# A 31-tap depthwise convolution: five of eight channel tiles moved from VectorE, ScalarE and GpSimd to TensorE as two-phase Toeplitz products

## The chip, the cores and the metric

The kernel runs on one core of one Trainium2 chip. The metric is the device time of one execution of the whole program in microseconds (us). TensorE is PE (its weight loads are PEld), VectorE is DVE, ScalarE is ACT, GpSimd is POOL, and SyncE (SP) issues most of the transfers.

## What is computed

The program is a whole stack of layers on 512 tokens with a model width of 1024: one hybrid layer, then feed-forward layers and two other mixers. Only the hybrid layer is touched. Cut to what matters:

```python
def causal_depthwise_conv(u, w, b):                  # 31 taps, each channel for itself
    y = lax.conv_general_dilated(u, w[:, None, :], window_strides=(1,),
        padding=[(CONV_SIZE - 1, 0)], dimension_numbers=("NWC", "WIO", "NWC"), feature_group_count=c)
    return y + b

def hybrid_layer(x, ...):
    h = rms_norm(x, pre_g)
    proj = jnp.einsum("bld,de->ble", h, w_in)
    conv_in, z_c, u_s, z_s, g_c, g_s = jnp.split(proj, IN_OFFSETS, axis=-1)
    ca, cb = jnp.split(conv_in, 2, axis=-1)
    cu = causal_depthwise_conv(ca * jax.nn.sigmoid(cb), conv_w, conv_b)
    cu = jax.nn.silu(layer_norm(cu, conv_ln_g, conv_ln_b))
    conv_out = jnp.einsum("blc,cd->bld", cu * jax.nn.silu(z_c), w_conv_out)
    y = jax.nn.gelu(s5_mimo(u_s, ...))               # a state-space scan, 32 groups
    y = y * jax.nn.sigmoid(jnp.einsum("blc,ce->ble", y, w_glu) + b_glu)
    ssm_out = jnp.einsum("blc,cd->bld", y * jax.nn.silu(z_s), w_ssm_out)
    merged = jax.nn.sigmoid(g_c) * conv_out + jax.nn.sigmoid(g_s) * ssm_out
    return x + rms_norm(jnp.einsum("bld,de->ble", merged, w_out), post_g)
```

All of it is float32. A float32 product on PE is made as three products of rounded halves: high by high, low by high and high by low.

## The kernel before

Channels lie on the 128 partitions and the 512 tokens on the free axis, so the 1024 conv channels are eight tiles of 128x512. The hybrid layer is `block1` (L598).

**Projections.** `wload` (L211) brings weights in pieces of 128x1024: SP issues a transfer of 512 KB into `raw` (L219; two buffers), ACT rounds it into `wh` (L220), and DVE subtracts to get `wl` (L221), with two buffers each. `mm3` (L226) then issues eight times the three products L232, L233, L234 for a piece, each 128x512, so a piece is 24 products. `proj(i)` makes two output tiles from two pieces.

**The conv.** For a tile, `pair` (L666) projects both halves and writes the gated input `cu` with 30 zeros ahead of it. `conv` (L683) has two forms. Tiles 0, 3, 4 and 5 (`CONV_POOL`) go to ACT and POOL: for each of the 30 further taps ACT makes `cw` (the shifted input times one weight, L689; two buffers), and POOL adds it to the sum (L690). Tiles 1, 2, 6 and 7 go to DVE: one multiply (L692) and 30 multiply-adds (L695). POOL sums the finished tiles into `sacc` (L699, L701). The layer norm starts with a PE product of `sacc` (L765, `ln`).

**The state-space scan (S5).** Tables come first on DVE (L342, L453, L457), then for each of four quarters `s5_pre` (Q: powers by L506 to L511 on DVE, products of tables on POOL at L488 and L491, small fp32 products on PE) and `s5_main` (q: PE products L556, L560, L568, L578, L579, with the scan L562 to L574 on DVE between them).

**What sets the order.** `run` (L800) walks two strings, ORDER_A (L902) and ORDER_B. A letter is a step and a digit its number: p is `pair`, c is `conv`, u, s and z are other projections, Q and q the scan, y the GELU behind it, g the gates, G the GLU, L the layer norm, S and C the two output products. B1_PRIO gives the conv (class C) a priority number 20000 higher, that is, the scheduler treats it as a filler. A list scheduler then fixes one static order for every engine; every engine works its list strictly in that order.

```python
ORDER_A = "p0 p1 T z0 c1 u0 u1 s0 p2 Q0 Q1 q0 c2 c0 p3 c3 s1 Q2 q1 p4 z1 Q3 q2 p5 p7 z2 q3 c5 c7 c4 p6 c6 z3"
ORDER_B = "y0 g0 g1 g2 y1 y2 y3 g3 G L g4 g5 g6 S0 g7 S1 C0 C1 C2 C3 C4 C5 C6 C7"
```

Of the kernel before, what the change touches and what calls it, by code (L numbers as in the profile page):

```python
# [1921 lines left out]
```

## Time and profile before

| | |
|---|---|
| three runs | 2721.5, 2722.85, 2728.67 us (median 2722.85) |
| the profiled execution | span 2722.4 us; no time of its own is listed beside the span |
| PE busy | 2562.2 us (94%) |
| DVE busy | 1551.5 us (57%) |
| ACT busy | 937.7 us |
| POOL busy | 593.6 us |
| transfers | 241.33 MB, 89 GB/s |

The hybrid layer takes the first 640 us or so of the span. The profile is one execution as the hardware recorded it. Busy time of PE is modelled from pipelined instructions, so the distance between the starts of products tells more than their durations. "x120" is a count, the number behind it a mean in ns, and "idle ... <-" the time an engine stood still ahead of such instructions and who ended it.

### The profile page before, as it was taken

Reading aid. Unit: us, or ns where it says so; the run is one execution under the profiler, and the core shown is the slowest. Engines: PE = TensorE matmul, PEld = TensorE weight load, DVE = VectorE, ACT = ScalarE, POOL = GpSimd, SP = SyncE. Lnnn points to the kernel's source line nnn. Section 1 sums busy time; section 2 is a strip of 40 time slices with the busy share of each in tenths; the row PEclk is TensorE's granted clock in tenths of the full one; section 3 lists DMA queues with packets and bytes.
Section 4 is the critical chain, followed back from the end, with each engine's and each line's share of the span. In section 5 each row is a group of like instructions: output and inputs, shape, how many; then the busy total and the mean of one; then the engine's idle time right before and its main releaser. Section 6 shows DMA issues by size and latency. Waiting matters only on the chain.

```text
span 2722.4 us, 31415 instructions
## 1 busy us (share of the span) xinstructions
PE 2562.2 (94%) x12356; PEld 2034.6 (75%) x12356; DVE 1551.5 (57%) x2148; ACT 937.7 (34%) x1337; POOL 593.6 (22%) x407
## 2 busy tenths in 40 slices
PE   6676778998999999999999999999999999999999
PEld 4565656887888876787678888888888666788887
DVE  9999897646434458653564344443444755643442
ACT  5343445443222333222243233322223554422231
POOL 5787765013000044432010000100001321100000
PEclk8888878998999999899999999999999989999999
DMA  3222112332222242213122322322324312122323
GB/s 112 68 64 64 58 63 81 105 112 70 96 98 101 91 146 64 65 57 111 63 93 90 104 93 92 102 99 88 104 88 134 118 41 66 55 95 88 106 94 106
DMA packets 113189, 241.33 MB, mean 89 GB/s; under 512 B 43856, under 2 KB 52688, under 8 KB 113040
## 3 DMA queue, kind: packets, MB, share of 16 engines
q1 hardware_dynamic: 112784, 238.52, 26.9%
q8 instruction: 97, 1.59, 0.2%
q0 software_dynamic: 256, 0.80, 0.1%
q14 instruction: 52, 0.43, 0.1%
HBM read 224.72 MB, written 13.37 MB: 87 GB/s over the span
## 4 chain that ended last, share of the span: by engine, by line
PE 77%; DVE 17%; issue 2%; DMA 1%; ACT 1%; POOL 1%; SPq 0%; DVEq 0%; ACTq 0%; POOLq 0%
PE bank L232 22%; PE bank L234 22%; PE bank L233 22%; DVE xa L695 4%; PE bank L1797 2%; DVE wl L221 2%; DVE s5x L342 1%; DVE kt L530 1%; ACT wh L220 1%; POOL acc L249 1%; PE bank L1349 1%; PE bank L1153 0%; DMA raw<-in_ffn_dn_dram 0%; DVE ra L509 0%; DVE s5t L342 0%
## 5 line engine op out<-in xcount | busy, mean ns | idle before, releaser
L234 PE MATMUL bank<-xh,wl 128*128 128x512 f32 (+1 forms) x2144 | 855.2, 399 | 69.7 <-DVE wl L221 69.3
L232 PE MATMUL bank<-xh,wh 128*128 128x512 f32 (+1 forms) x2144 | 849.1, 397 | 25.2 <-ACT wh L220 14.8
L233 PE MATMUL bank<-xl,wh 128*128 128x512 f32 (+1 forms) x2144 | 850.8, 397 | 15.7 <-DVE xl L851 6.9
L220 ACT CAST wh<-raw 128x1024 fp32r<-128x1024 f32 (+1 forms) x432 | 416.0, 964 | 1174.4 <-PE bank L233 941.4
L221 DVE TENSOR_TENSOR wl<-raw,wh 128x1024 fp32r<-128x1024 f32 (+2 forms) x398 | 459.6, 1156 | 385.7 <-ACT wh L220 384.4
L234 PEld LDWEIGHTS bank<-xh,wl 128*128 128x128 f32 x2144 | 414.1, 193 | 172.7 <-DVE wl L221 78.1
L232 PEld LDWEIGHTS bank<-xh,wh 128*128 128x128 f32 x2144 | 413.7, 193 | 119.2 <-ACT wh L220 19.9
L233 PEld LDWEIGHTS bank<-xl,wh 128*128 128x128 f32 x2144 | 414.2, 193 | 109.7 <-DVE xl L851 7.8
L249 POOL TENSOR_TENSOR acc<-acc,sq 128x512 f32<-128x512 f32 x54 | 81.5, 1509 | 1263.9 <-ACT sq L248 1263.0
L234 PE MATMUL bank<-mh,wl 128*128 128x512 f32 x704 | 274.4, 390 | 0.6 <-DVE wl L221 0.6
L233 PE MATMUL bank<-ml,wh 128*128 128x512 f32 x704 | 274.3, 390 | 0.0
L232 PE MATMUL bank<-mh,wh 128*128 128x512 f32 x704 | 274.1, 389 | 0.0
L308 DVE TENSOR_TENSOR up<-bank,rs 128x512 f32<-128x512 f32 x88 | 60.8, 691 | 267.2 <-PE bank L234 267.2
L690 POOL TENSOR_TENSOR xa<-xa,cw 128x512 f32<-128x512 f32 x120 | 191.3, 1595 | 56.4 <-ACT cw L689 51.7
L304 DVE TENSOR_TENSOR gp<-bank,rs 128x512 f32<-128x512 f32 x88 | 60.7, 690 | 180.1 <-PE bank L234 180.0
L234 PEld LDWEIGHTS bank<-mh,wl 128*128 128x128 f32 x704 | 132.1, 188 | 33.7 <-DVE wl L221 2.0
L233 PEld LDWEIGHTS bank<-ml,wh 128*128 128x128 f32 x704 | 132.2, 188 | 27.8
L232 PEld LDWEIGHTS bank<-mh,wh 128*128 128x128 f32 x704 | 132.2, 188 | 25.6
L695 DVE SCALAR_TENSOR_TENSOR xa<-cu,hcw,xa 128x512 f32<-128x512 f32 x120 | 141.8, 1181 | 1.6
L689 ACT ACTIVATE cw<-cu,hcw 128x512 f32<-128x512 f32 x120 | 85.3, 720 | 90.1 <-POOL xa L690 89.9
L221 POOL TENSOR_TENSOR wl<-raw,wh 128x1024 fp32r<-128x1024 f32 x34 | 82.7, 2434 | 145.9 <-ACT wh L220 145.4
L238 ACT CAST mh<-m 128x512 fp32r<-128x512 f32 x88 | 54.9, 624 | 60.8 <-DVE m L310 60.8
(636 smaller groups left out, 2836.7 us busy)
## 6 DMA issues: line engine op xcount, KB each, us to landing
raw<-in_ffn_gu_dram SPq DMA_DIRECT2D x176, 512.0 KB, 3.6
raw<-in_ffn_dn_dram SPq DMA_DIRECT2D x64, 512.0 KB, 3.5
raw<-in_w_in_dram SPq DMA_DIRECT2D x46, 512.0 KB, 3.6
raw<-in_even_in_dram SPq DMA_DIRECT2D x26, 512.0 KB, 3.6
raw<-in_ffn_dn_dram SPq DMA_DIRECT2D x64, 192.0 KB, 3.2
xa<-in_xT_dram SPq DMA_DIRECT2D x16, 256.0 KB, 4.4
raw<-in_w_co_dram SPq DMA_DIRECT2D x8, 512.0 KB, 3.3
raw<-in_w_out_dram SPq DMA_DIRECT2D x8, 512.0 KB, 3.5
```

The lines of the kernel that those rows point to most:

```text
L220: nc.scalar.copy(h[:, :m], raw[:, :m])
L221: self.wlo.tensor_tensor(out=l[:, :m], in0=raw[:, :m], in1=h[:, :m].bitcast(F32), op=ALU.subtract)
L232: self.nc.tensor.matmul(ps, h[i][:, s], xh[k], start=a, stop=False)
L233: self.nc.tensor.matmul(ps, h[i][:, s], xl[k], start=False, stop=False)
L234: last = self.nc.tensor.matmul(ps, l[i][:, s], xh[k], start=False, stop=b)
L238: self.nc.scalar.copy(hi, src)
L249: nc.gpsimd.tensor_tensor(out=acc, in0=acc, in1=sq, op=ALU.add)
L304: nc.vector.tensor_tensor(out=gp, in0=pg, in1=rs, op=ALU.mult)
L308: nc.vector.tensor_tensor(out=up, in0=pu, in1=rs, op=ALU.mult)
L689: A.activation(w, cu[:, j:j + T], AF.Copy, scale=hcw[:, 31 * k + j:31 * k + j + 1])
L690: GP.tensor_tensor(out=y, in0=y, in1=w, op=ALU.add)
L695: STT(out=y, in0=cu[:, j:j + T], scalar=hcw[:, 31 * k + j:31 * k + j + 1], in1=y, op0=ALU.mult, op1=ALU.add)
```

## The change

Tiles 1, 2, 4, 6 and 7 (`CONV_PE`) get their convolution from PE; tiles 0, 3 and 5 stay on ACT and POOL; DVE convolves nothing. For a tile on PE the tokens are split into even and odd ones (two phases), and 64 channels by two phases fill the 128 partitions. A tap pair is then a 128x128 matrix whose four blocks are diagonal: 16 such matrices for each group of 64 channels, 32 for a tile. The host lays them out as a new input `conv2` of 5x128x4096 floats (10.5 MB more to load).

- `phases(k)` (step P) does what `pair` did, with four 64x256 multiply-adds on DVE that write the two-phase layout `cp`, then a rounding on ACT (`cph`), a subtraction on DVE (`cpl`) and two small clears on POOL.
- `toeplitz(k)` (step t, class V, priority 0) loads four pieces of 128x1024 of `conv2` through the same `wload`, issues 96 products of 128x256 into a PSUM bank of its own (`cv`), and ACT writes the result back to token order in four 64x256 pieces.
- z2 and z3 move from ORDER_A to the front of ORDER_B; the side banks go from four to three; buffers of `zp` go from 12 to 8 with four in a new pool, and `CU_BUFS` from 3 to 2.

```diff
+CONV_PE = (1, 2, 4, 6, 7)
+        P.use_banks(mm=4, sd=3, cv=1)
+        def phases(k):
+            ...
+            cp = m_("cp")
+            va, cc = (x.rearrange("p (k o) -> p o k", o=2) for x in (vb, ca))
+            for g in range(2):
+                for o in range(2):
+                    gs = slice(64 * g, 64 * g + 64)
+                    STT(out=cp[64 * o:64 * o + 64, 256 * g:256 * g + 256], in0=va[gs, o], scalar=1.0, in1=cc[gs, o],
+                        op0=ALU.add, op1=ALU.mult)
+            hi, lo = (cup.tile([128, 2, 272], R, name=n, tag="cph", bufs=4) for n in ("cph", "cpl"))
+            for t in (hi, lo):
+                GP.memset(t[:, :, 0:16].bitcast(F32), 0.0)
+            c3 = cp.rearrange("p (g k) -> p g k", g=2)
+            A.copy(hi[:, :, 16:], c3)
+            TT(out=lo[:, :, 16:], in0=c3, in1=hi[:, :, 16:].bitcast(F32), op=ALU.subtract)
+            cus[k] = hi, lo
+        def toeplitz(k):
+            (hi, lo), y = cus[k], yc[k]
+            ps = P.bank("cv")
+            src = ap["conv2"][CONV_PE.index(k)]
+            for c in range(4):
+                (h,), (l,) = P.wload(src[:, 1024 * c:1024 * c + 1024], 1024)
+                g, s0 = c // 2, 8 * (c % 2)
+                for i in range(8):
+                    s = 16 - s0 - i
+                    o = slice(128 * i, 128 * i + 128)
+                    ...
+                    xh, xl = hi[:, g, s:s + 256], lo[:, g, s:s + 256]
+                    nc.tensor.matmul(d, h[:, o], xh, start=a, stop=False)
+                    nc.tensor.matmul(d, h[:, o], xl, start=False, stop=False)
+                    nc.tensor.matmul(d, l[:, o], xh, start=False, stop=b)
+            y3 = y.rearrange("p (k o) -> p o k", o=2)
+            for g in range(2):
+                for o in range(2):
+                    ps_ = slice(64 * o, 64 * o + 64)
+                    A.activation(y3[64 * g:64 * g + 64, o], ps[ps_, 256 * g:256 * g + 256], AF.Identity, scale=0.5, ...)
+            summed(k)
-ORDER_A = "p0 p1 T z0 c1 u0 u1 s0 p2 Q0 Q1 q0 c2 c0 p3 c3 s1 Q2 q1 p4 z1 Q3 q2 p5 p7 z2 q3 c5 c7 c4 p6 c6 z3"
-ORDER_B = "y0 g0 g1 g2 y1 y2 y3 g3 G L g4 g5 g6 S0 g7 S1 C0 C1 C2 C3 C4 C5 C6 C7"
-CU_BUFS = 3
-CONV_POOL = (0, 3, 4, 5)
+ORDER_A = "p0 P1 T z0 c0 u0 u1 s0 p3 t1 Q0 Q1 q0 c3 P2 t2 s1 Q2 q1 p5 z1 c5 P4 t4 Q3 q2 P6 t6 q3 P7 t7"
+ORDER_B = "z2 z3 y0 g0 g1 g2 y1 y2 y3 g3 G L g4 g5 g6 S0 g7 S1 C0 C1 C2 C3 C4 C5 C6 C7"
+CU_BUFS = 2
+CONV_POOL = (0, 3, 5)
```

The lines of the scan functions stand 15 lower in the new file (L221 is L236, L690 is L759). Up to the layer norm the PE list has 36 pieces of projections and GLU from u0 on in both kernels, and the new one has 20 pieces of `conv2` besides.

**TensorE, the seam between the projection of tile 7 and its convolution (step P7 to t7), in the new list.** `xh` and `xl` are the rounded halves of the layer's input, bank_80 is `cv`:

```order
L249 MATMUL bank_76<-xh_98,wl 128x512
L247 MATMUL bank_76<-xh_99,wh 128x512
L248 MATMUL bank_76<-xl_107,wh 128x512
L249 MATMUL bank_76<-xh_99,wl 128x512
L741 MATMUL bank_80<-cph,wh 128x256
L742 MATMUL bank_80<-cpl,wh 128x256
L743 MATMUL bank_80<-cph,wl 128x256
```

The first Toeplitz product stands directly behind the last projection product that its own input is made from; the 96 of tile 7 are followed by z2.

**VectorE, the scan of the first quarter (q0), before.** The scan is `vr`, `vs`, `st` (later `sh`); `xa` is the conv's output:

```order
L562 TENSOR_TENSOR vr<-bank_79,rsn 128x512
L563 TENSOR_TENSOR vs<-vs,rc 128x512
L695 SCALAR_TENSOR_TENSOR xa<-cu,hcw,xa 128x512
L221 TENSOR_TENSOR wl<-raw,wh 128x1024
L564 TENSOR_TENSOR vs<-vs,vr 128x512
L695 SCALAR_TENSOR_TENSOR xa<-cu,hcw,xa 128x512
L530 SCALAR_TENSOR_TENSOR kt<-ident,s5d,kt 16x16 x4
L566 SCALAR_TENSOR_TENSOR st_1229<-d_1202,vs 128x512
L695 SCALAR_TENSOR_TENSOR xa<-cu,hcw,xa 128x512 x2
L221 TENSOR_TENSOR wl<-raw,wh 128x1024
L695 SCALAR_TENSOR_TENSOR xa<-cu,hcw,xa 128x512
L678 SCALAR_TENSOR_TENSOR cu<-vb,bank_75 128x512
```

**The same place in the new list:**

```order
L545 SCALAR_TENSOR_TENSOR kt<-ident,s5d,kt 16x16 x4
L236 TENSOR_TENSOR wl<-raw,wh 128x1024 x2
L577 TENSOR_TENSOR vr<-bank_79,rsn 128x512
L578 TENSOR_TENSOR vs<-vs,rc 128x512
L579 TENSOR_TENSOR vs<-vs,vr 128x512
L581 SCALAR_TENSOR_TENSOR st_1945<-d_1918,vs 128x512
L236 TENSOR_TENSOR wl<-raw,wh 128x1024
L697 SCALAR_TENSOR_TENSOR cu<-vb,bank_75 128x512
L587 TENSOR_TENSOR vr<-bank_77,rsn 128x8x63
L588 TENSOR_TENSOR st_1945<-st_1945,rc 128x8x63
L515 MEMSET rsn 128x8
L589 TENSOR_TENSOR sh<-st_1945,vr 128x8x63
```

The conv's multiply-adds are gone from between the scan's steps. Splits of weights (L236) stand there, and the scan runs to its end (`sh`, which PE waits for) within these rows.

**ScalarE, the middle of the scan of the first quarter, before:**

```order
L689 ACTIVATE cw<-cu,hcw 128x512 x3
L220 CAST wh<-raw 128x1024
L689 ACTIVATE cw<-cu,hcw 128x512
L527 COPY kt<-bank_77 16x512
L689 ACTIVATE cw<-cu,hcw 128x512
L220 CAST wh<-raw 128x1024
L689 ACTIVATE cw<-cu,hcw 128x512
L675 ACTIVATE vb<-bank_76 128x512
L517 COPY m_1667<-bank_78 128x512
L689 ACTIVATE cw<-cu,hcw 128x512
L686 ACTIVATE xa<-cu,vec,hcw 128x512
L689 ACTIVATE cw<-cu,hcw 128x512 x2
```

**In the new list, from the load of the projection for P2:**

```order
L235 CAST wh<-raw 128x1024
L758 ACTIVATE cw<-cu,hcw 128x512 x4
L235 CAST wh<-raw 128x1024
L712 ACTIVATE vb<-bank_76 128x512
L532 COPY m_1869<-bank_77 128x512
L758 ACTIVATE cw<-cu,hcw 128x512 x2
L532 COPY m_1869<-bank_78 128x512
L724 CAST cph<-cp 128x2x256
L758 ACTIVATE cw<-cu,hcw 128x512 x5
L596 COPY yq<-bank_79 128x512
L758 ACTIVATE cw<-cu,hcw 128x512
L235 CAST wh<-raw 128x1024
```

In both lists roundings of weights (`wh`) stand behind runs of one to five `cw`; in the new one the tanh (L712) and rounding (L724) of `phases` stand among them too.

## Rows read from the trace of the kernel before

**Rows 1.** The page, parts 1 and 2: busy time of the engines; VectorE in 40 slices.

```profile
PE 2562.2 (94%) x12356; PEld 2034.6 (75%) x12356; DVE 1551.5 (57%) x2148; ACT 937.7 (34%) x1337; POOL 593.6 (22%) x407
...
DVE  9999897646434458653564344443444755643442
```

**Rows 2.** Windows: us, PE, PEld, DVE, ACT, POOL busy, clock, DMA share, GB/s.

```profile
59.40:140.30 80.90, 56.10 (x217) 43.12 (x217) 80.90 (x148) 28.44 (x38) 58.94 (x40) 0.82 0.22 71
...
237.00:290.30 53.30, 38.47 (x177) 30.98 (x176) 49.20 (x66) 23.21 (x36) 41.58 (x33) 0.81 0.21 60
...
374.20:444.00 69.80, 55.31 (x222) 44.66 (x222) 62.16 (x56) 36.68 (x57) 42.78 (x27) 0.83 0.24 80
...
59.40:444.00 384.60, 286.38 (x1192) 223.66 (x1192) 364.38 (x484) 160.02 (x229) 285.18 (x188) 0.84 0.21 65
444.00:608.00 164.00, 160.63 (x731) 131.73 (x729) 86.20 (x104) 70.54 (x98) 22.55 (x14) 0.98 0.30 103
```

**Rows 3.** Timeline of PE around 444: start, us, instruction.

```profile
443.98 1.02 PE L765 MATMUL bank<-sacc,ones 128*128 128x512 f32 x2
```

**Rows 4.** Groups of instructions, 59.4 to 444 us: busy, mean ns, idle before.

```profile
L690 POOL TENSOR_TENSOR xa<-xa,cw 128x512 f32<-128x512 f32 x120 | 191.3, 1595 | 56.4 <-ACT cw L689 51.7
L695 DVE SCALAR_TENSOR_TENSOR xa<-cu,hcw,xa 128x512 f32<-128x512 f32 x120 | 141.8, 1181 | 1.6
L234 PE MATMUL bank<-xh,wl 128*128 128x512 f32 x281 | 125.4, 447 | 64.6 <-DVE wl L221 64.6
...
L221 DVE TENSOR_TENSOR wl<-raw,wh 128x1024 fp32r<-128x1024 f32 x38 | 58.8, 1548 | 10.5 <-ACT wh L220 10.5
L220 ACT CAST wh<-raw 128x1024 fp32r<-128x1024 f32 x37 | 38.5, 1040 | 48.1 <-PE bank L233 33.3 <-DVE xa L695 7.2 <-DMA raw<-in_w_in_dram 4.9
L488 POOL TENSOR_TENSOR t<-s5bb,s5t 128x512 f32<-128x512 f32 x8 | 23.0, 2891 | 2.1 <-PE bank L516 2.1
...
L578 PE MATMUL bank<-us,tz 128*128 128x64 f32 x64 | 14.6, 316 | 2.6 <-ACT kt L527 2.6
...
L508 DVE TENSOR_TENSOR rc<-ra 128x8 f32<-128x8 f32 (+5 forms) x24 | 14.1, 594 | 0.3
...
L488 POOL TENSOR_TENSOR w<-s5c,s5t 128x576 f32<-128x576 f32 x6 | 8.5, 1436 | 0.0
L507 DVE TENSOR_TENSOR ra<-rsn,s5t 128x8 f32<-128x8 f32 (+5 forms) x24 | 7.7, 323 | 0.0
```

**Rows 5.** The conv's output tiles, 59 to 444 us: duration ns min/median/max.

```profile
L690 POOL TENSOR_TENSOR xa<-xa,cw x120: 1260/1597/4583, 64.0 to 436.8; 128x512 f32<-128x512 f32 x120
L695 DVE SCALAR_TENSOR_TENSOR xa<-cu,hcw,xa x120: 712/752/1897, 73.0 to 429.9; 128x512 f32<-128x512 f32 x120
```

**Rows 6.** The split weights, same stretch: duration ns min/median/max.

```profile
L221 DVE TENSOR_TENSOR wl<-raw,wh x38: 1205/1215/2305, 60.9 to 442.5; 128x1024 fp32r<-128x1024 f32 x38
```

**Rows 7.** Window of the conv's VectorE line L695 alone: us, DVE busy.

```profile
59.40:140.30 80.90, 30.33 (x30) 0.82 0.22 71
```

**Rows 8.** Timeline of PE: 512- and 256-column products.

```profile
594.91 0.39 PE L234 MATMUL bank<-xh,wl 128*128 128x512 f32 x1
595.14 0.28 PE L232 MATMUL bank<-xh,wh 128*128 128x256 f32 x1
595.25 0.28 PE L233 MATMUL bank<-xl,wh 128*128 128x256 f32 x1
```

**Rows 9.** Groups by form, 600 to 640 us: half-size tiles on ACT and DVE.

```profile
L851 DVE SCALAR_TENSOR_TENSOR xl<-xa,vec,xh 128x256 fp32r<-128x256 f32 x16 | 9.3, 605 | 2.5 <-ACT xh L850 2.5
...
L850 ACT ACTIVATE xh<-xa,vec 128x256 fp32r<-128x256 f32 x16 | 8.1, 505 | 11.5 <-POOL xa L848 11.5
```

**Rows 10.** Waits, 59.4 to 444 us: total, times, longest.

```profile
ACT cw L689 <- POOL xa L690: 89.9, 58, 8.8
...
POOL xa L690 <- ACT cw L689: 51.7, 18, 10.0
```

**Rows 11.** The page, part 6: transfers of weights; KB each, us to landing.

```profile
raw<-in_w_in_dram SPq DMA_DIRECT2D x46, 512.0 KB, 3.6
```

More of the change, by code (lines that the diff above doesn't have):

```diff
@@ L92, in pack @@
     put("invf", np.tile(invf, 4)[:, None])
+    cw = a["conv_w"][0].reshape(31, 8, 2, 64)
+    two = np.zeros((8, 2, 64, 2, 16, 2, 64), np.float32)
+    ch = np.arange(64)
+    for pi in range(2):
+        for po in range(2):
+            for s in range(16):
+                lag = 2 * s + po - pi
+                if 0 <= lag <= 30:
+                    two[:, pi, ch, :, s, po, ch] = cw[30 - lag].transpose(2, 0, 1)
+    f["conv2"] = two.reshape(8, 128, 4096)[list(CONV_PE)]
+    for k in range(8):
+        for g in range(2):
+            cb = a["conv_b"][0][128 * k + 64 * g:128 * k + 64 * g + 64]
+            vec[:, VEC["cb2"][0] + 2 * k + g] = np.concatenate([cb, cb])
     f["vec"] = vec
@@ L627, in z_, with y_ @@
             return zp.tile([128, T], dt, name=name, tag="z")
+        def y_(name, dt=F32):
+            return pools["z"].tile([128, T], dt, name=name, tag="z")
         def m_(name):
@@ L681, in block1 @@
         ndone = []
+        def phases(k):
+            if k < RAW:
+                (pa, pb), ca = pre[k], m_("ca")
+                vb = m_("vb")
+                TT(out=vb, in0=pb, in1=rs, op=ALU.mult)
+                A.activation(vb, vb, AF.Tanh, scale=0.5)
+                TT(out=ca, in0=pa, in1=rs, op=ALU.mult)
+            else:
+                ca, pb = proj(k)
+                vb = m_("vb")
+                A.activation(vb, pb, AF.Tanh, scale=0.5)
+            cp = m_("cp")
[12 more added lines that the diff above has]
+            cus[k] = hi, lo
@@ L717, in zc_ @@
             for a, ps in enumerate(proj(12 + i)):
-                z = z_("zc")
+                z = (z_ if i < 2 else y_)("zc")
                 A.activation(z, ps, AF.Silu)
@@ L776, in ln @@
                 TT(out=yc[k], in0=yc[k], in1=zc[k], op=ALU.mult)
-                f = z_ if k < 6 else c
+                f = z_ if k < 4 else y_ if k < 6 else c
                 a, b = f(f"cah{k}", R), f(f"cal{k}", R)
@@ L792, in block1 @@
         tb = {}
-        step = {"p": pair, "c": conv, "u": u_, "s": zs_, "z": zc_, "g": gate, "y": gelu,
+        step = {"p": pair, "c": conv, "P": phases, "t": toeplitz, "u": u_, "s": zs_, "z": zc_, "g": gate, "y": gelu,
                 "Q": lambda q: s5_pre(P, tb, q), "q": lambda q: s5_main(P, tb, q, u_dram, y_dram),
@@ L1883, in odd @@
         P.use_banks(mm=4, sd=4)
-_ORDER = ["xT", "vec", "w_in", "w_co", "w_so", "w_glu", "w_out", "s5p", "s5bc", "s5d", "ffn_gu", "ffn_dn",
+_ORDER = ["xT", "vec", "conv2", "w_in", "w_co", "w_so", "w_glu", "w_out", "s5p", "s5bc", "s5d", "ffn_gu", "ffn_dn",
           *EVEN_IN, *ODD_IN]
```

17 lines of the change are left out of this document (13 added, 4 removed).

## The prediction, made before the changed kernel was run

> **What bounds the kernel now.** I read the page first: PE is busy 94% of the span, but VectorE stands at nine tenths or more in the first slices and at half of that later [rows 1]. So the hybrid layer has a limit of its own, and PE's 94% is an average over others. Then the table of windows: from 59.4 us (the first piece of u0) to 444 us DVE is busy 364.4 of 384.6 us, while PE has gaps and a granted clock of 0.84; from 444 to 608 us PE is busy 160.6 of 164 us at 0.98 [rows 2]. The border is the layer norm's PE product [rows 3]: in front of it DVE sets the pace, behind it PE. In the groups the conv is DVE's largest line, 141.8 us, and PE stood idle 64.6 us ahead of L234 for DVE's split `wl` [rows 4]. So a conv multiply-add that leaves DVE lets the splits come earlier, and PE's time up to 444 us is what the change can move. What stands behind the norm is the same work in both kernels, limited by PE already, and keeps its length.
>
> The sum therefore asks one thing: when is the norm's product reached? It is made against the profiled execution, span 2722.4 us; the page gives no other time of it, and the median of the runs is 0.45 us higher. A measurement of this kernel tells about 0.3%, 8 us, from no change.
>
> **DVE and POOL part by part.** DVE loses 120 multiply-adds, 141.8 us, and 4 starts. It gains 20 splits, between 1.2 us (the fastest [rows 6]) and 1.55 us (the mean [rows 4]), so 24 to 31 us; 20 multiply-adds of 64x256, for which no row exists: the half tile of 128x256 took 0.605 us [rows 9], half that would be a floor, I take 0.5 us, 10 us in all (less five `cu` that fall away); and five subtractions, 3 us. Net it loses about 105 us. POOL loses 30 adds, ACT 30 `cw`. ACT gains 20 roundings of 1.04 us [rows 4], 20 evictions and 5 roundings at 0.5 us [rows 9]; at 160 of 384.6 us busy [rows 2] it is not the limit by its sum.
>
> An add on POOL takes 1.595 us in the mean, 1.26 at best; the multiply-add on DVE 1.181 in the mean, 0.712 at best [rows 4, 5]. Both are long while the other runs. With DVE's conv gone I take the middle for the add, 1.43 us, and keep 1.26 and 1.595 as ends.
>
> **PE.** Products of 512 columns start 0.227 us apart at full clock; two 256-column products, each with another weight, 0.11 us apart (0.12 over a longer stretch) [rows 8]. I take 0.12 us. Five tiles of 96 make 480 products, 58 us. The 36 other pieces up to the norm are 864 products, 196 us, in both kernels. The scan's small products I put at 60 us in both: some 260 records at the 0.23 us of L578 [rows 4]. So PE's work up to the norm rises from 256 to 314 us at full clock, with 384.6 us in which to do it before. That alone does not forbid a gain, but leaves at most 70 us of it.
>
> **The sum by stretches of the new order.** In each I price every engine and take the busiest; durations as above, the scan's POOL operations (46 in six lines, means from 1.44 to 2.89 us [rows 4]) at 1.8 us, the powers on DVE (six lines of 24, means 0.32 to 0.59 us [rows 4]) at 0.46 us.
> - u0 u1 s0 p3 (8 pieces): DVE was busy all 80.9 us of this stretch, 30.3 of them the conv [rows 2, 7]. Without these 50; but 72 powers stand here instead of 31: 41 x 0.46 = 19. DVE 69, POOL 17 x 1.43 + 16 x 1.8 = 53, PE 192 x 0.227 + 1.5 = 45. **69.**
> - t1 P2 t2 (10 pieces): POOL 28 x 1.43 + 16 x 1.8 + 3 = 72; PE 48 x 0.227 + 192 x 0.12 + 21 of scan = 55; DVE some 55. **72.**
> - s1 p5 z1 P4 (8): PE 43.6 + 17 = 61; POOL 51; DVE 40. **61.**
> - t4 P6 (6): PE 10.9 + 11.5 + 14 = 36; POOL 30. **36.**
> - t6 P7 t7 (10): PE 10.9 + 23 + 7 = 41, and two places where the first Toeplitz product waits for its own input: tanh, four multiply-adds, rounding, subtraction, 0.6 + 2 + 0.5 + 0.6 us and the hand-overs, 4.5 us each. **50.**
> - z2 z3 g0 to g3, GLU (14): 336 x 0.227 = 76, at PE's share behind the norm (160.6 of 164 [rows 2]) **78.**
>
> The first four are 238 us. Two corrections have opposite signs. Engines wait for each other: stretches in which DVE was not quite full took 53.3 us for 49.2 of its work and 69.8 for 62.2 [rows 2], 8 and 12% more. But the lists run over the borders, and over the four stretches no engine has more than 200 us (PE 197). I take neither. The norm is then reached at 59.4 + 238 + 50 + 78 = 425 us in place of 444, 19 us earlier: 2722.4 - 19 = **2704 us** (about 0.7% faster).
>
> The 10.5 MB of `conv2` cost nothing by bandwidth: transfers take 0.21 of the DMA engines there [rows 2]. By latency they have no slack: 3.6 us to land [rows 11], 1.04 to round, 1.2 to 1.55 to split, over two buffers, is about 3.0 us per piece, and PE eats a Toeplitz piece in 24 x 0.12 = 2.9 us. z2 and z3 cost nothing by moving: PE has them behind t7 with nothing else to wait for. The two small clears of `phases` on POOL and the third side bank I also put at nothing; POOL's slack in the last two stretches covers the clears.
>
> **The rivals.**
>
> 1. *It gains more, 2682 us.* If the lists overlap well, the four stretches take half-way between the largest sum of one engine (197) and 238, 218 us; the norm comes 39 us earlier with 50 and 78 as above, and 40 if the two waits shrink a little. For it: DVE no longer fills any stretch but the first. Against: PE's 314 us of work would have to fit into 345 (0.91), where before 256 took 384.6 (0.67) and my own sum has 366 (0.86).
>
> 2. *POOL and DVE take turns, 2740 us, slower.* The distance between best and mean on both engines [rows 5] can be read so that one of the two stands whenever the other reads two tiles. Then their times add: 88 adds at 1.26 (111), 46 scan operations at 1.44 (66), 32 splits at 1.2 (39), 148 powers at 0.32 (48) and some 10 us of the scan make 274 us for the four stretches in place of 238, and the norm comes at 461, 17 us late. It decides from a sum above 257, where the norm is where it was. Against it: the same sum before is 120 x (1.26 + 0.712) + 66 + 38 x 1.2 + 46 + 10 = 404 us, which did not fit into the 384.6 us that it took, so at least 20 us did overlap; and the median multiply-add took 0.752 us [rows 5], hardly more than the fastest.
> The Trainium skill, page "SBUF — State Buffer", section "Who interferes with whom", states this rule: a VectorE instruction with two SBUF inputs contends with a GpSimd instruction that reads SBUF, and who comes second is blocked for the whole instruction. The long instructions here agree with it, the 404 us do not agree with its strict form. By the rule the time would be rival 2's, and three conv tiles that stay on POOL would keep the new splits waiting.
>
> 3. *ACT's list starves PE, 2753 us, slower.* ACT's `cw` already waits 89.9 us for POOL [rows 10], and in the new list weight roundings stand behind up to five `cw`. Five adds on POOL are 8 us, a Toeplitz piece only 2.9, and there are two buffers. If waiting costs the worst ratio above in all four stretches (12%, 29 us) and every one of the 20 Toeplitz pieces comes 1 us late, that is 49 us against my sum, 30 us slower than before. Against it: POOL has fewer adds, and ACT has slack.
>
> 4. *Gain and loss cancel, about 2723 us.* Waiting at 8% in the four stretches takes back 19 us exactly. That the change would not do what it says I count here: the new lists show no conv instruction on DVE and all 480 Toeplitz products, so hardly 1 in 100.
>
> **How the numbers follow.** My forecast has a chance of 0.42, rival 1 0.08, rival 4 0.20, rival 2 0.17, rival 3 0.13. So faster 0.50, same 0.20, slower 0.30. Cases of both signs hold the chance; the forecast's own range is 2694 to 2714: adds at 1.26 us in the second stretch (5 us less) and splits at 1.2 us in the first and third (5 less) below, waits of 4% in the four stretches (10 us) above. The range for 8 in 10 reaches from 5 us under rival 1 (those adds again), 2677, to just above rival 3, 2757.
>
> **What would show it.** Right: DVE no longer near full between 59 and 425 us; L759 (the adds) nearer to 1.4 than 1.6 us; Toeplitz products 0.12 us apart at full clock within a piece; the norm's product, now L838, near 425 us; the 164 us behind it unchanged. The sum by stretches is wrong if z2 is reached much later than 347 us (59.4 + 238 + 50), and the place where PE stands then names the rival: for `wl` behind long splits, rival 2; for `wh` behind `cw`, rival 3. Wrong altogether would be a stretch behind the norm that changed its length.

## The result and the profile after

The changed kernel takes 2733.48 us (median of 6 runs) against 2721.78 us of before (6 runs): slower by some 12 us. The recorded ratio is 1.0052 with the interval 1.0033 to 1.007 (the medians alone give 1.0043). The forecast was 2704 us, faster; the wide range held the time, the sign was wrong. The profiled execution is the slowest of the six runs (2744.4 us, span 2742.7), 11 us above their median, while the profiled execution of before lies 1 us above its own; so the two profiles differ by 20 us where the medians differ by 12. Where I compare traces I look at single stretches and waits.

The page: busy time, then VectorE in 40 slices.

```profile
span 2742.7 us, 32329 instructions
...
PE 2610.5 (95%) x12836; PEld 2092.4 (76%) x12836; DVE 1447.9 (53%) x2064; ACT 950.4 (35%) x1351; POOL 511.4 (19%) x382
...
DVE  9967643636434448743464344443444755643443
```

Against [rows 1] PE has 48 us more, DVE 104 us and POOL 82 us less. The first slices of DVE are still at nine tenths. The timeline of PE shows the norm's product:

```profile
461.77 1.02 PE L838 MATMUL bank<-sacc,ones 128*128 128x512 f32 x2
```

It starts 17.8 us later than in [rows 3]; behind it the span has 2280.9 us left, before 2278.4. So the loss stands where the prediction put the gain, ahead of the norm. The windows of the six stretches (each runs from the rounding of its first piece to that of the next stretch's), then the whole up to the norm and a window of 164 us behind it; columns as in [rows 2]:

```profile
59.40:137.50 78.10, 52.90 (x207) 41.14 (x207) 77.17 (x171) 29.16 (x38) 54.57 (x42) 0.80 0.23 72
137.50:217.60 80.10, 60.63 (x343) 51.68 (x341) 57.66 (x83) 38.55 (x57) 62.81 (x51) 0.79 0.27 80
217.60:269.70 52.10, 52.10 (x266) 42.83 (x265) 33.35 (x40) 31.02 (x44) 43.79 (x34) 1.00 0.32 96
269.70:317.80 48.10, 35.62 (x212) 30.40 (x211) 38.10 (x49) 25.57 (x40) 34.14 (x28) 0.82 0.27 77
317.80:382.30 64.50, 51.63 (x292) 45.92 (x291) 31.67 (x43) 22.36 (x33) 6.73 (x6) 0.81 0.36 107
382.30:461.80 79.50, 79.50 (x364) 66.29 (x364) 23.26 (x23) 27.21 (x37) 1.29 (x1) 1.00 0.31 106
59.40:461.80 402.40, 332.38 (x1674) 278.26 (x1674) 261.22 (x405) 173.87 (x245) 203.33 (x160) 0.87 0.29 90
461.80:625.80 164.00, 157.46 (x733) 130.35 (x731) 89.58 (x108) 74.34 (x106) 28.14 (x21) 0.99 0.31 103
```

By these the stretches took 78, 80, 52, 48, 65 and 80 us, where the sum had 69, 72, 61, 36, 50 and 78; the third, 9 us shorter, hid a part of what the others lost. z2 is reached at 382 us in place of 347. DVE is full in the first stretch only. In the second no engine is above 63 of 80 us. The clock is granted fully (2.4 GHz) in the third and the last and is at 0.79 to 0.82 in the other four; if only 2.4 and 1.2 GHz occur, that is some 40% of them at 1.2 GHz. The groups, 59.4 to 461.8 us (busy, mean ns, idle before):

```profile
L759 POOL TENSOR_TENSOR xa<-xa,cw 128x512 f32<-128x512 f32 x90 | 129.1, 1435 | 55.1 <-ACT cw L758 52.5
L249 PE MATMUL bank<-xh,wl 128*128 128x512 f32 x281 | 113.9, 405 | 25.2 <-DVE wl L236 25.2
...
L236 DVE TENSOR_TENSOR wl<-raw,wh 128x1024 fp32r<-128x1024 f32 x58 | 81.0, 1397 | 107.3 <-ACT wh L235 107.3
...
L741 PE MATMUL bank<-cph,wh 128*128 128x256 f32 x160 | 51.0, 319 | 14.8 <-ACT cph L724 14.8
...
L521 DVE TENSOR_TENSOR ra<-rc,s5t 128x8 f32<-128x8 f32 (+5 forms) x24 | 16.9, 706 | 0.3
...
L524 DVE TENSOR_TENSOR ra<-rsn,s5t 128x8 f32<-128x8 f32 (+5 forms) x24 | 9.9, 414 | 0.4
```

PE's idle time for the splits of projections (L249) fell from 64.6 us [rows 4] to 25.2, as the change would have it; what is left stands in the first stretch. New is the idle time ahead of the Toeplitz products. The adds (L759) became shorter than in [rows 4], 1.435 us. The powers of the scan (first and last of six lines) became longer: the six lines sum to 84.1 us, 70.2 before. The waits:

```profile
ACT cw L758 <- POOL xa L759: 37.3, 41, 3.3
...
PE bank L249 <- DVE wl L236: 25.2, 5, 12.1
ACT cph L724 <- DVE cp L718: 19.8, 3, 9.8
...
PE bank L741 <- ACT cph L724: 14.8, 2, 9.0
...
PE bank L743 <- DVE wl L236: 10.9, 3, 9.5
```

ACT waits 37 us for POOL in place of the 89.9 of [rows 10]; PE waits 14.8 us for `cph` and 10.9 us for the split of a Toeplitz piece. For a rounding `wh` PE doesn't wait, and for POOL 0.6 us.

Of the 10.9 us one hole of 9.5 stands inside t2, behind 50 of its 96 products. Its timeline (start, us, engine, instruction, idle before):

```profile
202.50 1.04 ACT L235 CAST wh<-raw 128x1024 fp32r<-128x1024 f32 x1 [0.99 <-PE bank L742]
...
204.56 1.26 POOL L759 TENSOR_TENSOR xa<-xa,cw 128x512 f32<-128x512 f32 x1
204.71 1.19 DVE L523 TENSOR_TENSOR rc<-ra 128x64 f32<-128x64 f32 x1
...
210.75 1.34 DVE L522 TENSOR_TENSOR ra<-rsn,s5t 128x128 f32<-128x128 f32 x1
212.02 1.21 DVE L236 TENSOR_TENSOR wl<-raw,wh 128x1024 fp32r<-128x1024 f32 x1
213.15 0.28 DVE L523 TENSOR_TENSOR rc<-ra 128x128 f32<-128x128 f32 x1
...
213.28 0.58 PE L743 MATMUL bank<-cph,wl 128*128 128x256 f32 x1 [9.47 <-DVE wl L236]
```

The piece is rounded at 203.54, but its split stands in DVE's list behind seven powers, which take 1.0 to 1.34 us each: every one runs beside an operation of POOL (an add or a table product) and ends within 0.2 us of it. Behind them, with POOL standing, a power of the same 128x128 takes 0.28 us. So this hole is made by DVE and POOL taking turns, not by the place of P2 before t2.

The longest wait for a tile's own input is in front of t4:

```profile
287.03 1.22 DVE L236 TENSOR_TENSOR wl<-raw,wh 128x1024 fp32r<-128x1024 f32 x1
288.16 1.71 DVE L718 SCALAR_TENSOR_TENSOR cp<-vb,bank 64x256 f32<-64x256 f32 x4
...
289.90 0.62 ACT L724 CAST cph<-cp 128x512 fp32r<-128x512 f32 x1 [9.78 <-DVE cp L718]
...
290.57 0.58 PE L741 MATMUL bank<-cph,wh 128*128 128x256 f32 x1 [9.00 <-ACT cph L724]
...
291.77 2.63 POOL L759 TENSOR_TENSOR xa<-xa,cw 128x512 f32<-128x512 f32 x2 [9.70 <-ACT cw L758]
...
293.57 0.41 PE L743 MATMUL bank<-cph,wl 128*128 128x256 f32 x1
...
293.78 0.41 PE L741 MATMUL bank<-cph,wh 128*128 128x256 f32 x1
```

DVE's list has 16 powers and two splits between the tanh of P4, which ended at 276.3 us, and its `cp`; four of the powers, beside POOL's adds, took 1.2 to 1.4 us. ACT stood 9.78 us in front of `cph`, with two `cw` behind it, so POOL stood 9.70 us as well; PE stood 9.00 us. When PE goes on, its products start 0.21 us apart, at a granted clock of 0.50 (1.2 GHz). Here the clock had fallen already at 278, when PE ran the scan's small products with gaps; in t2's hole and in that before t7 it was 1.00 at the start and 0.50 at the end. So a hole is paid as idle time and as a low clock behind it, and the one before t4 also as adds that POOL could not do in it.

### The profile page after: what moved, and what is told of

Its sections match the earlier page's. It is cut to its first block, busy times and chain, and to the rows that moved or that the text cites. A ratio compares the mean times of both kernels' runs of the same rounds, so it can differ in the third digit from the quotient of the medians.

```text
span 2742.7 us, 32329 instructions
## 1 busy us (share of the span) xinstructions
PE 2610.5 (95%) x12836; PEld 2092.4 (76%) x12836; DVE 1447.9 (53%) x2064; ACT 950.4 (35%) x1351; POOL 511.4 (19%) x382
## 4 chain that ended last, share of the span: by engine, by line
PE 82%; DVE 12%; DMA 1%; issue 1%; ACT 1%; POOL 1%; SPq 1%; DVEq 0%; ACTq 0%; POOLq 0%
PE bank L247 23%; PE bank L249 23%; PE bank L248 23%; PE bank L1871 2%; DVE wl L236 2%; DVE s5x L357 1%; POOL acc L264 1%; SPq L548 1%; PE bank L1423 1%; PE bank L1227 0%; DVE ra L525 0%; PE bank L742 0%; PE bank L743 0%; DMA s<-nd 0%; DVE rc L523 0%
## 5 line engine op out<-in xcount | busy, mean ns | idle before, releaser
L235 ACT CAST wh<-raw 128x1024 fp32r<-128x1024 f32 (+1 forms) x452 | 437.2, 969 | 1268.1 <-PE bank L248 948.4
L249 PE MATMUL bank<-xh,wl 128*128 128x512 f32 (+1 forms) x2144 | 843.0, 394 | 30.0 <-DVE wl L236 30.0
L247 PE MATMUL bank<-xh,wh 128*128 128x512 f32 (+1 forms) x2144 | 838.2, 392 | 18.5 <-ACT wh L235 7.8
L236 DVE TENSOR_TENSOR wl<-raw,wh 128x1024 fp32r<-128x1024 f32 (+1 forms) x418 | 481.9, 1154 | 484.3 <-ACT wh L235 482.9
L249 PEld LDWEIGHTS bank<-xh,wl 128*128 128x128 f32 x2144 | 408.9, 191 | 125.6 <-DVE wl L236 33.7
L247 PEld LDWEIGHTS bank<-xh,wh 128*128 128x128 f32 x2144 | 408.0, 191 | 109.2 <-ACT wh L235 11.7
L248 PEld LDWEIGHTS bank<-xl,wh 128*128 128x128 f32 x2144 | 408.5, 191 | 106.2 <-DVE xl L925 7.8
L249 PE MATMUL bank<-mh,wl 128*128 128x512 f32 x704 | 274.6, 390 | 0.0
L249 PEld LDWEIGHTS bank<-mh,wl 128*128 128x128 f32 x704 | 132.1, 188 | 33.2 <-DVE wl L236 1.7
L759 POOL TENSOR_TENSOR xa<-xa,cw 128x512 f32<-128x512 f32 x90 | 129.1, 1435 | 55.1 <-ACT cw L758 52.5
L236 POOL TENSOR_TENSOR wl<-raw,wh 128x1024 fp32r<-128x1024 f32 x34 | 82.8, 2435 | 145.6 <-ACT wh L235 145.1
L758 ACT ACTIVATE cw<-cu,hcw 128x512 f32<-128x512 f32 x90 | 63.7, 720 | 37.5 <-POOL xa L759 37.3
L1871 PE MATMUL bank<-s,s 128*128 128x256 f32 (+3 forms) x192 | 71.6, 431 | 0.4 <-ACT s L1878 0.4
```

Source lines behind the costliest of these rows:

```text
L235: nc.scalar.copy(h[:, :m], raw[:, :m])
L236: self.wlo.tensor_tensor(out=l[:, :m], in0=raw[:, :m], in1=h[:, :m].bitcast(F32), op=ALU.subtract)
L247: self.nc.tensor.matmul(ps, h[i][:, s], xh[k], start=a, stop=False)
L248: self.nc.tensor.matmul(ps, h[i][:, s], xl[k], start=False, stop=False)
L249: last = self.nc.tensor.matmul(ps, l[i][:, s], xh[k], start=False, stop=b)
L758: A.activation(w, cu[:, j:j + T], AF.Copy, scale=hcw[:, 31 * k + j:31 * k + j + 1])
```

## The experiments

The times are medians; each ratio is to the kernel before, run on the same chip beside it. The medians of before there were 2721.1 to 2723.9 us, so a difference to the changed kernel's 2733.48 us is good to some 3 us. "Norm" is the start of the norm's product in the profile of that run. Behind the norm all kernels have the same steps, and yet the profiles have 2264 (no_cw) to 2282 us (no_pool) there; so the norm of a single profile tells less than the medians.

**seam.** Only the order of the steps P and t:

```diff
-ORDER_A = "p0 P1 T z0 c0 u0 u1 s0 p3 t1 Q0 Q1 q0 c3 P2 t2 s1 Q2 q1 p5 z1 c5 P4 t4 Q3 q2 P6 t6 q3 P7 t7"
+ORDER_A = "p0 P1 T z0 c0 u0 u1 s0 p3 t1 P2 Q0 Q1 q0 c3 t2 s1 Q2 q1 P4 p5 z1 c5 t4 P6 Q3 q2 P7 t6 q3 t7"
```

> Same work as the changed kernel; only the order string is altered, so that every step P (the input of a Toeplitz tile) stands at least one projection or one Toeplitz tile ahead of its own step t. Theory A (the loss sits in the holes where the first Toeplitz product waits for its own input, 9.7, 9.4 and 6.2 us before t2, t4 and t7, and in the low clock behind them): the holes go, the norm's product comes 15 to 25 us earlier, about 2713 us. Theory B (58 us more of PE work is the loss, holes or not): 2730 us or more. Theory C (ACT and POOL set the pace, PE's holes only show it): the holes move elsewhere, 2727 to 2736 us.

2713.06 us, ratio 0.9967 (0.9951 to 0.9983), 20 us less than the changed kernel; norm at 440.1 us. The window up to the norm, then all waits of PE's Toeplitz and projection products for DVE or ACT above 6 us:

```profile
59.40:440.10 380.70, 328.59 (x1675) 273.37 (x1674) 268.03 (x405) 172.46 (x245) 213.00 (x160) 0.91 0.31 95
```

```profile
PE bank L249 <- DVE wl L236: 31.9, 9, 10.0
...
PE bank L743 <- DVE wl L236: 6.8, 2, 5.7
```

The waits of L741 for `cph` are gone and the clock is at 0.91 in place of 0.87; waits for `wl` are about as in the changed kernel, and the powers took 80.5 us. The time is theory A's: the same work in another order turns a loss into a small gain. The 9.7 us before t2 in the expectation are the split's hole shown above.

**hi_only.** Two of the three Toeplitz products left out:

```diff
-                    nc.tensor.matmul(d, h[:, o], xh, start=a, stop=False)
-                    nc.tensor.matmul(d, h[:, o], xl, start=False, stop=False)
-                    nc.tensor.matmul(d, l[:, o], xh, start=False, stop=b)
+                    nc.tensor.matmul(d, h[:, o], xh, start=a, stop=b)
```

> The changed kernel with one of three products in the Toeplitz tiles (the products with the low halves are left out: 320 products, 38 us of PE at 0.12 us; loads, roundings and splits of the weights stay). Theory B (PE's work): the full 38 us come back, about 2695 us. Theory A (holes at the seams): the holes stay and grow by a part of it, 10 to 25 us come back, 2708 to 2723 us. Theory C (ACT and POOL): under 12 us, 2721 us or more.

2721.73 us, ratio 1.0004 (0.9988 to 1.0021): 12 us less than the changed kernel for 38 us of products. Where the rest went, from the waits up to its norm (448.6 us):

```profile
PE bank L249 <- DVE wl L236: 49.7, 11, 13.4
```

25.2 us in the changed kernel became 49.7: PE got done earlier and waited for DVE's splits. Theory B, that PE's added work is the whole loss, falls; the time lies in theory A's range and at the edge of C's and doesn't tell these two apart.

**no_pool, no_adds, no_cw.** The three POOL tiles without 29 of 30 taps; without the adds only; without the products on ACT only:

```diff
 # no_pool
-                for j in range(1, 31):
+                for j in range(1, 2):
 # no_adds
-                    GP.tensor_tensor(out=y, in0=y, in1=w, op=ALU.add)
+                    if j == 30:
+                        GP.tensor_tensor(out=y, in0=y, in1=w, op=ALU.add)
 # no_cw
-                    w = P.t("cw", "cw")
-                    A.activation(w, cu[:, j:j + T], AF.Copy, scale=hcw[:, 31 * k + j:31 * k + j + 1])
-                    GP.tensor_tensor(out=y, in0=y, in1=w, op=ALU.add)
+                    GP.tensor_tensor(out=y, in0=y, in1=cu[:, j:j + T], op=ALU.add)
```

> The changed kernel with 29 of the 30 further taps of each of the tiles 0, 3 and 5 left out (87 cw on ACT, 87 adds on POOL). Theory C (ACT's list behind POOL's adds sets the pace up to t4, 80 us in the second stretch of which POOL has 72): 25 to 40 us come back, under 2708 us. Theory A: the holes before t4 and t7 stay, 5 to 15 us, 2718 to 2728 us. Theory B: nothing, 2728 us or more.

> The changed kernel with the 90 products cw on ACT left out: POOL adds the shifted input itself, so all 90 adds run, read as much as before and wait for nothing on ACT, and ACT's list holds no cw. Leaving out the taps on both engines gave back 47 us. Theory C1 (the way is through ACT's list: weight roundings stand behind cw that wait for POOL): 30 us or more come back, under 2704 us. Theory C2 (POOL's adds lengthen DVE's splits, powers and tables while both run, and ACT's list only follows): under 15 us come back, 2718 us or more.

> The changed kernel with 29 of 30 adds of tiles 0, 3 and 5 left out on POOL and all 90 cw kept on ACT, which now wait for nobody. Theory C2 (contention of POOL with DVE): nearly all 47 us come back, 2686 to 2696 us. Theory C1: the waits of ACT go too, but its own 63 us of cw stay ahead of the roundings, 2696 to 2715 us.

no_pool 2686.23 us, ratio 0.9855 (0.9817 to 0.9893); no_adds 2681.33 us, 0.9847 (0.9819 to 0.9875); no_cw 2737.22 us, 1.0059 (1.0038 to 1.008). The adds are worth 52 us. The `cw` gave nothing back: with them out POOL runs on without ACT and the whole is as slow as the changed kernel, though POOL's denser adds may hide a few us there. So ACT's list was not the main way by which POOL costs time. The main way is DVE. The first stretch of no_adds, then the powers (the first and the last of the six lines by time) of no_adds, and L521 and L522 of no_cw:

```profile
59.40:119.60 60.20, 52.78 (x217) 40.27 (x218) 59.27 (x172) 35.93 (x52) 34.35 (x26) 0.91 0.31 95
```

```profile
L521 DVE TENSOR_TENSOR ra<-rc,s5t 128x8 f32<-128x8 f32 (+5 forms) x24 | 9.7, 402 | 0.3
...
L522 DVE TENSOR_TENSOR ra<-rsn,s5t 128x8 f32<-128x8 f32 (+5 forms) x24 | 5.7, 238 | 0.0
```

```profile
L521 DVE TENSOR_TENSOR ra<-rc,s5t 128x8 f32<-128x8 f32 (+5 forms) x24 | 19.7, 821 | 0.3
...
L522 DVE TENSOR_TENSOR ra<-rsn,s5t 128x8 f32<-128x8 f32 (+5 forms) x24 | 12.8, 536 | 0.0
```

Without the adds the six lines take 47.6 us in place of 84.1, and the first stretch, which DVE fills in both, 60 in place of 78 us. PE's waits for `wl` (L249 and L743) fall from 36.1 to 10.7 us. With POOL adding unpaced (no_cw) the lines take 91.0 us. A power alone needs 0.2 to 0.4 us; beside an operation of POOL it waits up to the length of one. Of the 144 powers 34 took over 0.9 us before, 48 in the changed kernel and 13 in no_adds, and none of those that ran with no long operation of POOL beside them took more than 0.43 us.

**bef_no_dve.** The kernel before without 29 of 30 multiply-adds of each DVE tile, the removing half of the change:

```diff
-                for j in range(1, 31):
+                for j in range(1, 2):
                     STT(out=y, in0=cu[:, j:j + T], scalar=hcw[:, 31 * k + j:31 * k + j + 1], in1=y,
```

> The kernel before with 29 of 30 multiply-adds of each of the four DVE tiles left out and nothing put in their place: the removing half of the change alone. DVE has some 222 us of work left up to the norm, PE 256 and POOL some 285 (less where contention goes). If the conv on DVE was the limit: the norm comes 70 to 110 us earlier, 2610 to 2650 us. Rival: POOL's 120 adds and ACT hold it, 30 to 60 us earlier, 2660 to 2690 us; then the changed kernel's 58 us of added PE work could hardly fit.

2670.61 us, ratio 0.9812 (0.9779 to 0.9846): in the rival's range, not in that of a kernel limited by DVE's conv alone. Taking 141.8 us of multiply-adds from an engine that was 95% busy gave 52 us; the 120 adds on POOL ran at 1.49 us then, and PE still waited 42.7 us for `wl`. The powers, first and last of six lines:

```profile
L510 DVE TENSOR_TENSOR ra<-rc,s5t 128x8 f32<-128x8 f32 (+5 forms) x24 | 16.7, 697 | 0.0
...
L511 DVE TENSOR_TENSOR rsn<-ra 128x8 f32<-128x8 f32 (+5 forms) x24 | 11.6, 500 | 0.4
```

The six sum to 83.9 us, 70.2 before: taking the conv from DVE alone makes the powers as long as they are in the changed kernel (84.1). What the change puts in the conv's place costs 63 us (2733.48 - 2670.61).

**half_toep, hi_nosplit.** Every second Toeplitz piece left out; hi_only without the splits of `conv2` on DVE:

```diff
 # half_toep
-            for c in range(4):
+            for c in (0, 2):
-                    a, b = s0 + i == 0, s0 + i == 15
+                    a, b = i == 0, i == 7
 # hi_nosplit, on top of hi_only
-                (h,), (l,) = P.wload(src[:, 1024 * c:1024 * c + 1024], 1024)
+                raw = P.wr.tile([128, 1024], F32, name="raw", tag="raw")
+                h = P.whp.tile([128, 1024], R, name="wh", tag="wh")
+                nc.sync.dma_start(raw, src[:, 1024 * c:1024 * c + 1024])
+                A.copy(h, raw)
```

> The changed kernel with every second piece of conv2 left out (half of the taps of the five PE tiles): 240 products fewer (29 us of PE) and 10 transfers, roundings and splits fewer. In hi_only 38 us of products alone gave 12 us. If feeding the pieces is what the Toeplitz tiles cost (a DVE split of 1.4 us and an ACT rounding of 1.05 each): 20 to 35 us come back, 2698 to 2713 us. If neither feed nor products set the pace: 6 to 14 us, 2719 to 2727 us.

> hi_only with the 20 splits of the conv2 pieces on DVE left out too (their low halves are used nowhere in it); transfers and roundings stay. hi_only gave 12 us for 38 us of products; half_toep gave 35 us for 29 us of products and ten feeds. If the splits on DVE, in line with powers that POOL lengthens, are what the feeding costs: 15 to 30 us more than hi_only, 2692 to 2707 us. If it is the transfers and roundings, or the number of pieces: 2714 to 2724 us.

half_toep 2698.79 us, ratio 0.99 (0.9873 to 0.9927); hi_nosplit 2709.03 us, 0.9952 (0.9936 to 0.9968). Ten feeds with 29 us of products gave 35 us, 38 us of products alone 12; the 20 splits gave 13 us more, less than the 15 I had as a floor but outside the other theory's range. If such prices add up, feeding a Toeplitz piece costs at least as much as its products, and DVE's splits are about half of what hi_only and hi_nosplit together gave. How the rest divides between transfer and rounding was not tried.

**late5, late5s.** The same numbers of tiles with other tiles: PE convolves 0, 1, 2, 6, 7, two of them early; POOL's 3, 4, 5 start late. late5s has P6 and P7 a step earlier too:

```diff
-CONV_PE = (1, 2, 4, 6, 7)
-CONV_POOL = (0, 3, 5)
+CONV_PE = (0, 1, 2, 6, 7)
+CONV_POOL = (3, 4, 5)
+ORDER_A = "P0 P1 T z0 u0 t0 u1 t1 s0 Q0 Q1 q0 p3 c3 P2 s1 Q2 q1 t2 p4 c4 z1 p5 c5 Q3 q2 P6 t6 q3 P7 t7"  # late5
+ORDER_A = "P0 P1 T z0 u0 t0 u1 t1 s0 Q0 Q1 q0 p3 c3 P2 s1 Q2 q1 t2 p4 c4 P6 z1 p5 c5 t6 Q3 q2 P7 q3 t7"  # late5s
```

> Five tiles on PE and three on ACT and POOL as in the changed kernel, 480 Toeplitz products and 90 adds, but tiles 0, 1, 2, 6, 7 on PE and 3, 4, 5 on POOL: PE convolves early, while DVE makes the tables and powers of the scan, and POOL's adds start after the first two quarters of them. Theory of contention (in the changed kernel the powers took 84 us, 48 without the adds): the powers take 50 to 65 us and the whole 2695 to 2712 us. Rival (POOL's adds only meet other DVE work later, and the holes before t6 and t7 are still there): 2720 to 2735 us.

> late5 with P6 and P7 a step ahead of t6 and t7. If contention (late5, 28 us) and holes at the seams (seam, 20 us) are separate losses: a part of the 20 us comes on top, some 10 us for two of the five tiles, 2692 to 2698 us. If both had removed the same loss: 2702 to 2708 us.

2705.52 us, ratio 0.9937 (0.9917 to 0.9957), and 2698.54 us, 0.9907 (0.9884 to 0.9931). The powers of late5, longest and shortest of the six lines:

```profile
L523 DVE TENSOR_TENSOR rc<-ra 128x8 f32<-128x8 f32 (+5 forms) x24 | 11.7, 502 | 0.3
...
L525 DVE TENSOR_TENSOR ra<-rc,s5t 128x8 f32<-128x8 f32 (+5 forms) x24 | 7.9, 329 | 0.0
```

They sum to 60.4 us. With all 480 Toeplitz products and all 90 adds the kernel is 28 us faster than the changed one, and late5s 7 more. Both times and the powers fit the theory of contention, but late5 isn't a test of it alone: its order also parts P2 from t2, and PE's waits of L741 for `cph` are 2.0 us there (5.0 in late5s) in place of 14.8. So the 28 us hold a part of seam's 20, how much was not tried, and what gave late5s its 7 us stays open.

**two_dve.** Tiles 6 and 7 back on DVE as fillers:

```diff
-CONV_PE = (1, 2, 4, 6, 7)
+CONV_PE = (1, 2, 4)
-ORDER_A = "p0 P1 T z0 c0 u0 u1 s0 p3 t1 Q0 Q1 q0 c3 P2 t2 s1 Q2 q1 p5 z1 c5 P4 t4 Q3 q2 P6 t6 q3 P7 t7"
+ORDER_A = "p0 P1 T z0 c0 u0 u1 s0 p3 t1 Q0 Q1 q0 c3 P2 t2 s1 Q2 q1 p5 z1 c5 P4 t4 Q3 q2 p6 c6 q3 p7 c7"
```

> The changed kernel with tiles 6 and 7 back on DVE as fillers (62 instructions, some 47 us at the 0.75 us that one takes while POOL stands) and only tiles 1, 2 and 4 on PE. PE loses 192 products (23 us) and two seams (some 6 us of holes and the low clock behind). Theories A and B: the norm's product comes some 30 us earlier, about 2700 us, faster than both kernels. Rival: the multiply-adds delay the splits of z2 to g3 and the layer norm waits for the last tile, 2722 us or more.

2694.28 us, ratio 0.9892 (0.9866 to 0.9919), the shortest median of those that compute everything (late5s has 2698.54 with an interval that overlaps); norm at 418.5 us. The multiply-adds there:

```profile
L764 DVE SCALAR_TENSOR_TENSOR xa<-cu,hcw,xa 128x512 f32<-128x512 f32 x60 | 44.2, 764 | 0.4
```

0.764 us in place of 1.181 [rows 4], since POOL starts its last add at 319.4 us and DVE its first multiply-add at 330.0: 44 us of DVE work stand there, and the kernel is 39 us faster than with the same two tiles, and their seams, on PE (2733.48 - 2694.28).

**combo, combo2, late3, late3l, four_one: misses.** Attempts to add the gains: two_dve with P2 and P4 a step early (combo; combo2 with p7 behind q3 in the string, which gave almost the same lists), late5's order with tiles 6 and 7 on DVE (late3; late3l with the DVE tiles last and in buffers of their own), late5s with tile 7 on DVE (four_one).

```diff
+ORDER_A = "p0 P1 T z0 c0 u0 u1 s0 p3 t1 P2 Q0 Q1 q0 c3 t2 s1 Q2 q1 P4 p5 z1 c5 t4 Q3 q2 p6 c6 p7 q3 c7"  # combo
+ORDER_A = "P0 P1 T z0 u0 t0 u1 t1 s0 Q0 Q1 q0 p3 c3 P2 s1 Q2 q1 t2 p4 c4 z1 p5 Q3 q2 c5 p6 c6 q3 p7 c7"  # late3
+ORDER_A = "P0 P1 T z0 u0 t0 u1 t1 s0 Q0 Q1 q0 p3 c3 P2 s1 Q2 q1 t2 p4 c4 P6 z1 p5 c5 t6 Q3 q2 p7 q3 c7"  # four_one
```

> Tiles 1, 2 and 4 on PE with every step P a step ahead of its own t (as in seam), tiles 6 and 7 on DVE (as in two_dve), tiles 0, 3 and 5 on ACT and POOL. Seam gave 20 us, two_dve 39, and two_dve still has holes of 10.3 and 8.7 us before t2 and t4. If these are what the order removes: 2675 to 2685 us. Rival: the holes in front of t2 are POOL's and DVE's doing, and the order only moves them: 2690 to 2698 us.

> combo with p7 put back behind the scan's last quarter, as in two_dve: combo's trace stands 10 us ahead of two_dve's up to 327 us and then loses 30 us at the scan of the last quarter, where PE has no projection left and DVE's list has conv multiply-adds between the steps of the scan. If that is the place: 2680 to 2688 us. Rival (a step P early costs as much elsewhere): 2690 us or more.

> Tiles 0, 1, 2 on PE early, 3, 4, 5 on ACT and POOL behind the first powers, 6 and 7 on DVE last: late5's contention and two_dve's division together. If the two add: 2655 to 2675 us, the fastest of all. Rival (the POOL tiles come late and the layer norm waits for them, or DVE's conv collides with them): 2690 to 2710 us.

> late3 (2712 us) with its two DVE tiles moved behind the scan's last quarter in the order string, and their inputs in the buffers that the Toeplitz tiles no longer need, so that p7 doesn't wait for POOL's tile 5. late3 lost 10.6, 7.6 and 11.8 us in three holes between 322 and 381 us. If those are the buffer and the multiply-adds between the scan's steps: 2680 to 2695 us. If the list still mixes them with the scan, or POOL's late tiles lengthen them: 2703 us or more.

> late5s (2698.5 us) with tile 7 on DVE in place of PE: 96 products, four feeds and the seam before t7 fall away (16 to 20 us by half_toep's price of 35 us for 10 feeds and 240 products), 31 instructions of some 0.75 us come to DVE. In its DVE list eight multiply-adds stand between the steps of the last quarter's scan and one to seven between the splits, as in combo. If one tile is short enough to hide: 2680 to 2690 us, the fastest. If the scan's last quarter waits behind them as in combo: 2697 us or more.

2710.14, 2707.27, 2712.25, 2711.63 and 2709.82 us (ratios 0.9962, 0.9933, 0.995, 0.9963, 0.9951): all faster than before, none as fast as its better parent (late3l is level with late3). In four_one the timeline of DVE and then of PE shows why:

```profile
339.99 11.87 DVE L764 SCALAR_TENSOR_TENSOR xa<-cu,hcw,xa 128x512 f32<-128x512 f32 x7
...
353.99 5.08 DVE L764 SCALAR_TENSOR_TENSOR xa<-cu,hcw,xa 128x512 f32<-128x512 f32 x3
358.99 0.68 DVE L577 TENSOR_TENSOR vr<-bank,rsn 128x512 f32<-128x512 f32 x1
...
363.60 1.21 DVE L581 TENSOR_TENSOR_SCAN st<-d,vs 128x512 f32<-128x512 f32 x1
```

```profile
346.16 0.40 PE L249 MATMUL bank<-xh,wl 128*128 128x512 f32 x1
364.86 2.08 PE L583 MATMUL bank<-st,perm 128*128 128x512 f32 x2 [18.30 <-DVE st L581]
```

Seven multiply-adds take 11.87 us, 1.7 each, because POOL's late adds run beside them, and they stand in DVE's list ahead of the scan's last quarter; PE has no projection left in its own list before that and stands 18.3 us. combo2 waits at the same place, 6.5 us for `st` and 3.8 us for `sh`, at a low clock. In two_dve the last quarter's products stand in the middle of projections.

## Why the prediction was wrong

- *What bounds the kernel:* right as to the place. What stands behind the norm kept its length (2278.4 and 2280.9 us), the time moved ahead of it, and DVE's conv was a limit: leaving it out gave 52 us. It was not the only one, as the rival's range in bef_no_dve shows.
- *Prices of single operations:* mostly right. The add came to 1.435 us (1.43 taken), the Toeplitz products start 0.12 us apart at full clock:

```profile
145.00 0.28 PE L741 MATMUL bank<-cph,wh 128*128 128x256 f32 x1
145.12 0.28 PE L742 MATMUL bank<-cpl,wh 128*128 128x256 f32 x1
```

  The multiply-adds of `phases` took 0.42 us where they read one input from PSUM and 1.12 where both lie in SBUF (0.5 taken).
- *The step that failed first:* "the powers on DVE ... at 0.46 us", a term of DVE's sum and of nothing else. I let the adds get shorter because DVE's conv went, and kept the mean of the powers, as if contention could only ease. It moved instead: without long multiply-adds in between, the powers took 0.584 us (84.1 us for 144), and bef_no_dve has the same 83.9 us with nothing put in. In the first stretch the price held (70 powers at 0.46 us); it took 78 in place of 69 us mostly by `cp` and `cpl` of P1 (5.2 us that the sum did not have), longer splits (14.1 for 11.8 us) and 31 powers that the 50 us already held at only 0.31 us each. In the second and fourth stretch the powers took 0.72 and 0.75 us. DVE was not full there; the loss is that splits and `cp` stand behind them, and PE stood 9.5 us inside t2.
- *The step that failed second:* "I take neither". The sum takes the busiest engine of each stretch, and the waits of engines for each other it prices at nothing, but for "two places where the first Toeplitz product waits for its own input ... 4.5 us each". These two came to 1.3 us (t6) and 6.4 (t7), less than priced. What it had at nothing was t4's hole of 9.0 us, since I added up the operations of `phases` and not what stands ahead of them in DVE's and ACT's lists, and the low clock. In all PE was idle for 70 of the 402 us up to the norm. The fourth stretch has 35.6 us of PE and 12.5 of waits. The fifth has 51.6 us of PE, about the 41 of the sum at a clock of 0.81 (41 / 0.81 = 51), and 12.9 of waits, 4.5 of them for a transfer (`us`). The two took 112.6 us in place of 86. The order alone gave back 20 us (seam).
- *The feed:* "by latency they have no slack" was seen and priced at nothing. half_toep and hi_nosplit show that it costs.
- *The rivals:* 2 was nearest, 2740 us by POOL and DVE taking turns, and its mechanism is the one that no_adds and no_cw bear out; of its sign, PE standing for `wl`, there were 36.1 us. In t2's hole it holds strictly, one power to each operation of POOL; over all it does not: the four stretches took 258 us, not 274. Its 148 powers should be 144, which changes its sum by 1 us. Of the Trainium skill's rule ("SBUF — State Buffer", "Who interferes with whom") the runs show the part that matters here: a small VectorE operation that reads two tiles waits beside POOL's adds. Rival 3 fell: PE did not wait for `wh`, and without the `cw` on ACT the kernel was no faster.
- *What is not shown:* how the 12 us divide between contention, the place of the steps P, and the feed. The gains of no_adds (52 us), seam (20) and half_toep (35) overlap and don't add up.

## What to carry to other kernels

When work leaves an engine that shares a resource, ask whom the remaining partner will meet next, and price the small operations at their contended length: here POOL's adds went from lengthening multiply-adds to lengthening the powers behind which the splits stand that PE waits for. Before paying for a new engine, look at when the old one is free: here two tiles on DVE, once POOL was done, left the kernel 39 us faster than the same two on PE. An operation that makes another engine's input belongs a step ahead of its use, and one has to read what stands before it in its own list.
